# A decoder layer on one Trainium2 core: a room for the first down weights, scores over 128 rows, and a reordered norm

## The chip, the cores and the metric

The kernel runs on one core of a Trainium2 chip. The metric is the time of one execution on the device, in microseconds (us); lower is better. A core has five engines with a queue of instructions each: PE (TensorE, matrix products), DVE (VectorE), ACT (ScalarE), POOL (GpSimd) and SP (SyncE, which here issues nearly all DMAs). An engine takes its instructions in the order in which they stand in its queue, and an instruction waits by semaphores for the results and buffers of other engines.

## The reference

One layer of a decoder for 520 columns: 512 positions of a prompt and one new position each of 8 running sequences. The model has width 1024. Two feed-forward parts of hidden width 2816 enclose a mixer.

```python
def half_ffn(x, g, w1, w3, w2):
    h = rmsnorm(x, g)
    return x + 0.5 * ((jax.nn.silu(h @ w1) * (h @ w3)) @ w2)

def trunk_layer(x, ffn1, mixw, ffn2, past):
    g_mix, w_in, conv_w, g_conv, g_attn, w_out = mixw
    x = half_ffn(x, *ffn1)
    h = rmsnorm(x, g_mix)
    ...
    y_c = rmsnorm(b_g * conv_out, g_conv)
    y_a = rmsnorm(attn.reshape(attn.shape[:2] + (ATTN_WIDTH,)), g_attn)
    x = x + jnp.concatenate([y_c, y_a], axis=-1) @ w_out
    x = half_ffn(x, *ffn2)
    return x, state
```

In the mixer `h @ w_in` gives the three inputs of a gated convolution (512 channels) and q, k, v of 8 heads of 64. The prompt's attention adds up three dilated windows, and the 8 running sequences look into a cache of 1024 positions, which is also copied to the output with the new rows. A last norm closes the program.

## The kernel before

All activations lie transposed: 1024 rows in 8 tiles `X` of 128 partitions, 520 columns in two halves of 260. A float32 operand is split into a high and a low part of a shorter format, and a product takes three matrix products (`mm3`, lines 121 to 123): high by high, high by the activation's low part, low by high. `load_w` (L95) brings a block of weights into `raw` by DMA, ACT makes `hi` of it (L108) and DVE makes `lo` (L109). `hi` and `lo` have three buffers each, `raw` four.

**Feed-forward parts** (`ffn`, L225). The first four hidden tiles are made with plain products, the other 18 in pairs (`pair`, L318), where `seven` (L366) forms two output tiles with seven products in place of eight, from sums of weight blocks; the sums' high and low parts are the tiles `hs` and `ls` in the pool `su` (L382), with two buffers each. The hidden tiles are `hh` and `hl` (L305, L334). The down projection `down` (L412) is run after the hidden tiles 0 to 3, 4 to 13 and 14 to 21 (`CUTS`), each time over all 8 output tiles, with its own weights from `load_w`, which it adds into `X`. Behind the last pair, `preload()` (L73) loads ACT's table that holds both logarithm and exponential. The Silu of the hidden tiles (L301, L324) uses another table; where an ACT function isn't in the table loaded last, the build puts a load ahead of it.

**Mixer.** Weights for the first three projections are loaded ahead (`ahead`, L497), then the operand `mh`, `ml` and the squares are made, and `rstd_rows` (L164) makes the norm's factor: it adds up the squares by a product with ones, DVE forms the mean (L182), ACT takes a logarithm and an exponential (L183, L184), and DVE refines the result (L185 to L187). The projections q, k, v, the convolution's parts, the heads and the cache's products run in an order written by hand (`ORDER`, L33); a timeline scheduler then mixes what is ready. `head` (L578) makes the scores of one head in eight products: four with 128 rows, in which the key tile `k2` holds its high part in one half of the rows and its low part in the other and the query's high part `q2` stands in both, and four with 64 rows for the query's low part `ql` with the key's high part. `rstd` (L189) is a norm by columns for the convolution's group (step R), with `rstd_columns` (L146) and `spread` (L157); `rstd_rows` once more is the attention group's norm (`r2`, L813), which `out_proj` needs at L771.

**End.** The second `down` with `finish` (L820) makes the last tiles half by half; each half runs `rstd_columns`, whose logarithm and exponential are L150 and L151, then `give` (L845): `spread`, the products with the norm's factor on DVE and POOL, and the DMAs out.

## Time and profile before

| | us |
|---|---|
| median of three runs | 1001.39 (1000.5 to 1004.54) |
| the profiled execution | 1001.53 |
| its span in the trace | 999.7 |
| PE busy | 977.4 (98%) |
| DVE busy | 719.6 (72%) |
| ACT busy | 519.9 (52%) |
| POOL busy | 69.7 (7%) |

The first feed-forward part lasts until about 373 us, the mixer until about 622, the second feed-forward part until about 977, and the last norm to the end. In the rows of a timeline, the first number is the start, the second the duration; a bracket at the end tells how long the engine had been idle and who ended that. The durations of PE's products overlap, so the distance of their starts is what counts.

### The profile page before, as it was taken

How to read it: one execution, taken by the hardware profiler on the slowest of the kernel's cores; microseconds unless marked ns; L12 is line 12 of the kernel's file. 1: busy time of each engine (PE TensorE's matmuls, PEld its weight loads, DVE VectorE, ACT ScalarE, POOL GpSimd, SP SyncE). 2: the span in 40 equal slices, each digit the busy share in tenths (PEclk: the TensorE clock that was granted, in tenths of full speed). 3: DMA queues.
4: the chain of work that ended last, by engine and by line, in shares of the span. 5: the costliest groups of instructions: out<-in, count | busy, mean ns of one | idle time of the engine just before them, and what ended most of it. 6: DMA issues, size and time to landing. Idle time of an engine off the chain costs nothing.

```text
span 999.7 us, 19200 instructions
## 1 busy us (share of the span) xinstructions
PE 977.4 (98%) x7897; PEld 955.6 (96%) x7897; DVE 719.6 (72%) x1153; ACT 519.9 (52%) x941; POOL 69.7 (7%) x89
## 2 busy tenths in 40 slices
PE   8999999999999999999999999999999999999997
PEld 8999999999999999999999899999999999999997
DVE  7889987336886446667788899769988634788432
ACT  5536665324665446667566555435656422565442
POOL 1000000000000131112022210000000000000022
PEclk9999999999999999999999999999999999999998
DMA  7344343445444444243146565325443233333302
GB/s 243 110 137 164 133 147 123 163 138 173 145 147 130 165 157 149 89 145 138 65 152 228 197 225 191 108 94 179 149 147 127 80 93 104 106 107 106 106 22 86
DMA packets 37912, 136.62 MB, mean 137 GB/s; under 512 B 5760, under 2 KB 8512, under 8 KB 37312
## 3 DMA queue, kind: packets, MB, share of 16 engines
q1 hardware_dynamic: 37824, 135.39, 39.9%
q8 instruction: 62, 1.02, 0.4%
q14 instruction: 26, 0.21, 0.1%
HBM read 131.07 MB, written 37.82 MB: 169 GB/s over the span
## 4 chain that ended last, share of the span: by engine, by line
PE 78%; DVE 11%; DMA 5%; issue 3%; ACT 2%; POOL 1%; SPq 0%; POOLq 0%; DVEq 0%; ACTq 0%
PE ps L121 24%; PE ps L123 24%; PE ps L122 24%; DVE lo L390 2%; DMA raw<-in_w3a 2%; PE s L589 1%; DMA raw<-in_w1a 1%; DVE ls L390 1%; DVE lo L109 1%; DMA raw<-in_w1b 1%; DVE raw L377 1%; PE pt L610 1%; DVE ws L378 1%; DVE ws L376 1%; DVE ws L375 1%
## 5 line engine op out<-in xcount | busy, mean ns | idle before, releaser
L108 ACT ACTIVATE hi<-raw 128x1024 fp32r<-128x1024 f32 (+3 forms) x136 | 119.0, 878 | 208.3 <-PE ps L122 162.7
L121 PE MATMUL ps<-hh,hi 128*128 128x260 f32 x704 | 198.4, 284 | 3.4 <-ACT hi L108 1.4
L123 PE MATMUL ps<-hh,lo 128*128 128x260 f32 x704 | 198.8, 284 | 1.2 <-DVE lo L109 1.2
L122 PE MATMUL ps<-hl,hi 128*128 128x260 f32 x704 | 198.2, 282 | 0.1
L109 DVE TENSOR_TENSOR lo<-raw,hi 128x1024 fp32r<-128x1024 f32 (+3 forms) x136 | 138.6, 1020 | 76.3 <-ACT hi L108 75.0
L121 PEld LDWEIGHTS ps<-hh,hi 128*128 128x128 f32 x704 | 132.3, 189 | 4.9 <-ACT hi L108 1.8
L123 PEld LDWEIGHTS ps<-hh,lo 128*128 128x128 f32 x704 | 132.2, 188 | 2.1 <-DVE lo L109 1.6
L122 PEld LDWEIGHTS ps<-hl,hi 128*128 128x128 f32 x704 | 132.6, 188 | 0.4 <-DVE hl L305 0.3
L121 PE MATMUL ps<-mh,hi 128*128 128x260 f32 x384 | 110.1, 287 | 1.7 <-DVE q L518 1.1
L123 PE MATMUL ps<-mh,lo 128*128 128x260 f32 x384 | 109.4, 285 | 0.2 <-DVE u L643 0.2
L122 PE MATMUL ps<-ml,hi 128*128 128x260 f32 x384 | 109.3, 285 | 0.0
L389 ACT ACTIVATE hi<-raw 128x512 fp32r<-128x512 f32 x144 | 82.9, 622 | 37.2 <-PE ps L122 27.9
L390 DVE TENSOR_TENSOR lo<-raw,hi 128x1024 fp32r<-128x1024 f32 x72 | 87.8, 1219 | 7.2 <-ACT hi L389 6.9
L123 PE MATMUL ps<-f1sh,lo 128*128 128x260 f32 x288 | 81.6, 285 | 1.8 <-DVE lo L390 1.7
L121 PE MATMUL ps<-f0sh,hi 128*128 128x260 f32 x288 | 81.8, 284 | 1.4 <-ACT a L405 1.0
L121 PE MATMUL ps<-f1sh,hi 128*128 128x260 f32 x288 | 81.5, 283 | 0.7 <-ACT a L405 0.5
L123 PE MATMUL ps<-f0sh,lo 128*128 128x260 f32 x288 | 81.3, 285 | 0.7 <-DVE lo L390 0.6
L122 PE MATMUL ps<-f0sl,hi 128*128 128x260 f32 x288 | 81.2, 282 | 0.0
L122 PE MATMUL ps<-f1sl,hi 128*128 128x260 f32 x288 | 81.1, 282 | 0.0
L144 POOL TENSOR_TENSOR acc<-acc,sq 128x520 f32<-128x520 f32 (+1 forms) x19 | 28.9, 1523 | 741.4 <-ACT sq L143 737.5
L121 PEld LDWEIGHTS ps<-mh,hi 128*128 128x128 f32 x384 | 72.4, 189 | 2.8 <-issue 1.8
L122 PEld LDWEIGHTS ps<-ml,hi 128*128 128x128 f32 x384 | 72.4, 188 | 1.1 <-issue 0.7
(278 smaller groups left out, 2664.5 us busy)
## 6 DMA issues: line engine op xcount, KB each, us to landing
out_cko<-in_ck SPq DMA_DIRECT2D x16, 1023.0 KB, 6.8
out_cvo<-in_cv SPq DMA_DIRECT2D x16, 1023.0 KB, 6.8
raw<-in_w_in SPq DMA_DIRECT2D x24, 512.0 KB, 3.3
raw<-in_w1b SPq DMA_DIRECT2D x22, 512.0 KB, 3.3
raw<-in_w3b SPq DMA_DIRECT2D x22, 512.0 KB, 3.3
raw<-in_w3a SPq DMA_DIRECT2D x21, 512.0 KB, 3.3
raw<-in_w1a SPq DMA_DIRECT2D x20, 512.0 KB, 3.3
raw<-in_w2a SPq DMA_DIRECT2D x16, 320.0 KB, 2.9
```

The lines of the kernel that those rows point to most:

```text
L108: A.activation(hi, raw, AF.Copy)
L109: V.tensor_tensor(lo, raw, hi.bitcast(F32), ALU.subtract)
L121: PE.matmul(out, lhsT=hi, rhs=xh, start=start, stop=False, skip_group_check=more)
L122: PE.matmul(out, lhsT=hi, rhs=xl, start=False, stop=False, skip_group_check=more)
L123: PE.matmul(out, lhsT=lo, rhs=xh, start=False, stop=stop, skip_group_check=more)
L144: eng.tensor_tensor(dst[:, c], dst[:, c], sq[:, c], ALU.add)
L375: V.tensor_tensor(s[:, 0], rb[:, :KQ], rb[:, KQ:], ALU.add)
L376: V.tensor_tensor(s[:, 1], s[:, 0], ra[:, :KQ], ALU.add)
L377: V.tensor_tensor(rb[:, :KQ], rb[:, :KQ], ra[:, :KQ], ALU.add)
L378: V.tensor_tensor(s[:, 2], s[:, 1], ra[:, KQ:], ALU.add)
L389: A.activation(h[:, c:c + KQ], f[:, c:c + KQ], AF.Copy)
L390: V.tensor_tensor(l, f, h.bitcast(F32), ALU.subtract)
```

## The change

- `load_w` can be given a `room`, two tiles into which it puts `hi` and `lo`. After the pairs of the second and the third group, `ffn` takes two more tiles of the pool `su`, of the size and tags of `hs` and `ls`, and loads the first weights of the following down projection into them (`down_weights`), ahead of `down`, and in the third group ahead of `preload()`.
- After the first four hidden tiles, the output tiles 0 and 1 run together (`late`): the products with the first three hidden tiles for both, then with the fourth for both.
- The scores take, for the query's low part too, 128 rows: each head's low part stands in a tile of 128 rows, of which the other 64 are zero. There are four such tiles, zeroed once by POOL, and each holds its half in turn. The eight products stand in plain order.
- The mixer's third weight is loaded behind the exponential of the norm. The zeros of `pth`, `ptl` and `sq2` are written by POOL; the tiles `sqm` of the cache's products share the slots of `q2`, and are taken once.
- In `ORDER`, step B0 comes ahead of q2.

```diff
-ORDER = ("A0 C00 C01! k1 q1 q2 B0 v1 v2 t1 C02 A1! B1! k3 k2 t2 A2 v3 C10 C11 q3 B2 t3 A3 C12 "
+ORDER = ("A0 C00 C01! k1 q1 B0 q2 v1 v2 t1 C02 A1! B1! k3 k2 t2 A2 v3 C10 C11 q3 B2 t3 A3 C12 "
...
-    def load_w(src, n, cuts=None, then=None):
+    def load_w(src, n, cuts=None, then=None, room=None):
         raw = wp.tile([P, n, P], F32, name="raw", tag="raw", bufs=4)
-        hi = wp.tile([P, n, P], F32R, name="hi", tag="whi")
-        lo = wp.tile([P, n, P], F32R, name="lo", tag="wlo")
+        hi, lo = room or (wp.tile([P, n, P], F32R, name=x, tag=f"w{x}") for x in ("hi", "lo"))
...
-        A.activation(out, out, AF.Exp, scale=-0.5)
+        power = A.activation(out, out, AF.Exp, scale=-0.5)
...
+        return power
...
-                for m, then in zip((0, 1, 4, 5, 2, 6, 3, 7), (sum_x, None, sum_x) + 5 * (None,)):
-                    down(w2, 0, CUTS[1], Hh, Hl, psum_tile, ms=(m,))
+                for ms, then in zip(((0, 1), (4,), (5, 2, 6, 3, 7)), (sum_x, sum_x, None)):
+                    down(w2, 0, CUTS[1], Hh, Hl, psum_tile, ms=ms, late=len(ms) == 2)
...
                 for m in range(c0, c1, 2):
                     pair(m)
+                room = [su.tile([P, 12, P], F32R, name=x, tag=x) for x in ("hs", "ls")]
+                first = down_weights(w2, c0, c1, 0, room)
                 if c1 < KF:
-                    down(w2, c0, c1, Hh, Hl, psum_tile)
+                    down(w2, c0, c1, Hh, Hl, psum_tile, first=first)
             preload()
...
-            down(w2, CUTS[-2], KF, Hh, Hl, psum_tile, finish)
+            down(w2, CUTS[-2], KF, Hh, Hl, psum_tile, finish, first=first)
...
+    def down_weights(w2, k0, k1, m, room=None):
 
         n = k1 - k0 if k1 - k0 <= KD else (k1 - k0) // 2
+        return [tuple(load_w(w2[m, :, k:k + n], n, room=room and [t[:, k - k0:k - k0 + n] for t in room])) + (k, n)
+                for k in range(k0, k1, n)]
...
+        if late:
+            ws, ps = [parts(m) for m in ms], [psum_tile() for m in ms]
+            for a, b in ((0, k1 - k0 - 1), (k1 - k0 - 1, k1 - k0)):
+                with tc.issue_after(PE_last()) if a else ExitStack():
+                    for w, p in zip(ws, ps):
+                        gemm(p, w, Hh, Hl, of=(a, b))
...
-            ahead = [load_w(w_in[mt], KD) for mt in (20, 12, 16)]
+            ahead = [load_w(w_in[mt], KD) for mt in (20, 12)]
...
-            rstd_rows(two, sums, D, rbc)
+
+            with tc.issue_after(rstd_rows(two, sums, D, rbc).ins):
+                ahead.append(load_w(w_in[16], KD))
...
-                V.memset(t[:, 0:128].bitcast(F32), 0.0)
+                G.memset(t[:, 0:128].bitcast(F32), 0.0)
...
+            rest = [[ap.tile([P, S], F32R, name=f"ql{i}{e}") for e in range(2)] for i in range(2)]
+            for r in rest:
+                for e in range(2):
+                    G.memset(r[e][ROWS[1 - e]].bitcast(F32), 0.0)
...
-                    V.tensor_tensor(ql[ROWS[e]], q[ROWS[e], :S], q2[e][ROWS[e]].bitcast(F32), ALU.subtract)
+                    V.tensor_tensor(ql[e][ROWS[e]], q[ROWS[e], :S], q2[e][ROWS[e]].bitcast(F32), ALU.subtract)
...
-                for at_, (ib, low) in enumerate(((0, 0), (1, 0), (0, 1), (1, 1), (2, 1), (2, 0), (3, 0), (3, 1))):
+                for ib in range(4):
...
-                    mm = PE.matmul(dst[ib], lhsT=ql[rows, i] if low else q2[e][:, i], rhs=k2[e][rows if low else slice(0, P), :n],
-                                   start=at_ in (0, 4, 6), stop=one or at_ in (5, 7), skip_group_check=one and at_ > 0)
...
+                    PE.matmul(dst[ib], lhsT=q2[e][:, i], rhs=k2[e][:, :n], start=True, stop=False)
+                    PE.matmul(dst[ib], lhsT=ql[e][:, i], rhs=k2[e][:, :n], start=False, stop=True)
...
+                if not zeroed:
+                    zeroed.extend(ap.tile([P, HP * 130 + 64], F32R, name=f"sqm{i}", tag=f"q2{i}", bufs=2) for i in range(2))
```

How instructions stand after the change is shown in three places. The line numbers of the new kernel differ by up to some twenty from those above. ACT, last pair of the first feed-forward part, before: L324 to L326 are the last pair's Silu, L397 to L405 its copies out of PSUM, L108 the first weights of the down projection, L334 the last hidden tiles, L75 the preload.

```order
L334 ACTIVATE hh_3625<-b 128x520
L389 ACTIVATE hi<-raw 128x512 x2
L324 ACTIVATE a<-a 128x520
L399 ACTIVATE b<-ps 128x260
...
L401 ACTIVATE b<-ps 128x260
L108 ACTIVATE hi<-raw 128x1024
L326 ACTIVATE a<-ps 128x260
L108 ACTIVATE hi<-raw 128x1024
L334 ACTIVATE hh_3875<-b 128x520
L405 ACTIVATE b<-ps 128x260
L108 ACTIVATE hi<-raw 128x1024
L334 ACTIVATE hh_3879<-b 128x520
L75 ACT_TABLE_LOAD
```

The same place now (L107 is the old L108; L391, L401, L403 and L407 are the old L389, L399, L401 and L405):

```order
L407 ACTIVATE b<-ps 128x260
L107 ACTIVATE hs<-raw 128x1024
L75 ACT_TABLE_LOAD
L403 ACTIVATE a<-ps 128x260
L391 ACTIVATE hi<-raw 128x512 x2
L334 ACTIVATE hh_3623<-b 128x520
L391 ACTIVATE hi<-raw 128x512 x2
L401 ACTIVATE b<-ps 128x260
L324 ACT_TABLE_LOAD
L324 ACTIVATE a<-a 128x520
```

The first weights now go to `hs`, ahead of the last pair's copies; the preload has moved with them, and the Silu brings a load of its own. The second feed-forward part reads alike.

ACT, the attention group's norm, before (L183 and L184 are its logarithm and exponential):

```order
L108 ACTIVATE hi<-raw 128x512
L171 ACTIVATE rhi<-acc_a 128x520
L108 ACTIVATE hi<-raw 128x512 x2
L183 ACTIVATE r_4475<-rv_7207 128x520
L184 ACTIVATE r_4475<-r_4475 128x520
L108 ACTIVATE hi<-raw 128x512 x2
```

The same place now (each line number is one less):

```order
L107 ACTIVATE hi<-raw 128x512
L170 ACTIVATE rhi<-acc_a 128x520
L107 ACTIVATE hi<-raw 128x512 x2
L182 ACT_TABLE_LOAD
L182 ACTIVATE r_4473<-rv_7207 128x520
L183 ACT_TABLE_LOAD
L183 ACTIVATE r_4473<-r_4473 128x520
L107 ACTIVATE hi<-raw 128x512 x2
```

Two table loads have come in; the same two stand at the norm ahead of the mixer, at the convolution's norm, at the norm ahead of the second feed-forward part, and twice at the last norm. In all, ACT has 19 table loads now, where it had 5.

PE, the first head's scores, before (`s01`, `s2` and `s3` are the sums of query blocks 0 and 1, 2, and 3):

```order
L589 MATMUL s01_4688<-k20_4668,q20_4599 128x256 x2
L589 MATMUL s01_4688<-k20_4668,ql_4601 128x256 x2
L589 MATMUL s2_4689<-k20_4668,ql_4601 128x384
L589 MATMUL s2_4689<-k20_4668,q20_4599 128x384
L589 MATMUL s3_4690<-k20_4668,q20_4599 128x512
L589 MATMUL s3_4690<-k20_4668,ql_4601 128x512
```

The same place now:

```order
L610 MATMUL s01_4693<-k20_4673,q20_4605 128x256
L611 MATMUL s01_4693<-k20_4673,ql00_4484 128x256
L610 MATMUL s01_4693<-k20_4673,q20_4605 128x256
L611 MATMUL s01_4693<-k20_4673,ql00_4484 128x256
L610 MATMUL s2_4694<-k20_4673,q20_4605 128x384
L611 MATMUL s2_4694<-k20_4673,ql00_4484 128x384
L610 MATMUL s3_4695<-k20_4673,q20_4605 128x512
L611 MATMUL s3_4695<-k20_4673,ql00_4484 128x512
```

High and low parts take turns now, all with the full tile `ql00`; in the other heads other products stand between some of the eight, in both kernels.

## Rows read from the trace of the kernel before

**Rows 1.** The page, part 1: each engine's busy time, share, instructions.
```profile
PE 977.4 (98%) x7897; PEld 955.6 (96%) x7897; DVE 719.6 (72%) x1153; ACT 519.9 (52%) x941; POOL 69.7 (7%) x89
```
**Rows 2.** Busy time by stretch: PE, PEld, DVE, ACT, POOL; PE's clock; DMA.
```profile
60.00:115.00 55.00, 54.15 (x446) 53.51 (x447) 53.58 (x78) 31.63 (x59) 0.00 (x0) 1.00 0.46 159
400.00:575.00 175.00, 174.35 (x1332) 162.96 (x1330) 134.05 (x286) 109.32 (x209) 32.43 (x54) 1.00 0.42 146
977.00:1000.00 23.00, 16.84 (x146) 16.37 (x145) 7.00 (x24) 5.33 (x14) 4.64 (x7) 0.83 0.28 94
```
**Rows 3.** Timeline of PE, the first head's scores: start, duration, instruction.
```profile
405.92 0.40 PE L589 MATMUL s<-k,q 128*128 128x256 f32 x2
...
407.46 0.49 PE L589 MATMUL s<-k,ql 64*128 64x512 f32 x1
407.88 0.40 PE L121 MATMUL ps<-mh,hi 128*128 128x260 f32 x1
408.11 0.29 PE L122 MATMUL ps<-ml,hi 128*128 128x260 f32 x1
```
**Rows 4.** Timeline of PE, products of 512 columns over 128 rows.
```profile
420.40 0.40 PE L619 MATMUL o<-pth,v 128*128 128x512 f32 x1
420.64 0.39 PE L621 MATMUL o<-ptl,v 128*64 128x512 f32 x1
```
**Rows 5.** Timeline of PE: its waits at the down projections of the first part.
```profile
59.87 0.39 PE L121 MATMUL ps<-hh,hi 128*128 128x260 f32 x1 [0.92 <-ACT hh L305]
...
188.96 0.39 PE L121 MATMUL ps<-hh,hi 128*128 128x260 f32 x1 [0.71 <-ACT hi L108]
...
323.67 0.39 PE L123 MATMUL ps<-hh,lo 128*128 128x260 f32 x1 [0.61 <-DVE lo L109]
...
330.00 0.39 PE L121 MATMUL ps<-hh,hi 128*128 128x260 f32 x1 [0.52 <-DVE b L330]
```
**Rows 6.** Timeline of ACT: table loads, and what follows one of them.
```profile
331.00 1.28 ACT L75 ACT_TABLE_LOAD   x1
...
641.31 1.28 ACT L301 ACT_TABLE_LOAD   x1
642.60 0.64 ACT L301 ACTIVATE a<-a 128x520 f32<-128x520 f32 x1
```
**Rows 7.** Timeline of ACT at the norm ahead of the mixer.
```profile
382.59 1.06 ACT L108 ACTIVATE hi<-raw 128x1024 fp32r<-128x1024 f32 x1 [4.59 <-PE ps L122]
...
384.57 0.62 ACT L184 ACTIVATE rbc<-rbc 128x520 f32<-128x520 f32 x1
```
**Rows 8.** Timeline of PE, mixer's start, and a product behind the attention's norm.
```profile
385.63 0.28 PE L121 MATMUL ps<-mh,hi 128*128 128x260 f32 x1
...
393.07 0.36 PE L121 MATMUL ps<-mh,hi 128*128 128x260 f32 x1 [1.07 <-DVE q L518]
...
399.71 0.36 PE L121 MATMUL ps<-mh,hi 128*128 128x260 f32 x1 [0.62 <-DVE k L518]
...
603.48 0.36 PE L121 MATMUL ps<-Yh,hi 128*128 128x260 f32 x1
```
**Rows 9.** Timeline of ACT at the attention group's norm.
```profile
597.75 0.63 ACT L108 ACTIVATE hi<-raw 128x512 fp32r<-128x512 f32 x1 [2.72 <-PE ps L122]
598.29 0.62 ACT L183 ACTIVATE r<-rv 128x520 f32<-128x520 f32 x1
598.95 0.64 ACT L184 ACTIVATE r<-r 128x520 f32<-128x520 f32 x1
```
**Rows 10.** Timeline of DVE: the first use of that norm.
```profile
602.64 0.70 DVE L771 TENSOR_TENSOR t<-ps,r 128x520 f32<-128x520 f32 x1
```
**Rows 11.** Waits of PE: who is waited for, us in all, times, longest.
```profile
PE nps L160 <- DVE rr L154: 0.3, 1, 0.3
```
**Rows 12.** Timeline of ACT: the last norm's two logarithms.
```profile
983.81 0.20 ACT L150 ACTIVATE rr<-rv 65x4 f32<-65x4 f32 x1 [2.20 <-DVE rv L149]
...
990.59 0.20 ACT L150 ACTIVATE rr<-rv 65x4 f32<-65x4 f32 x1 [0.37 <-DVE rv L149]
```

More of the change, by code (lines that the diff above doesn't have):

```diff
@@ L410, in seven, with down @@
         return px
-    def down(w2, k0, k1, Hh, Hl, psum_tile, finish=None, ms=range(KD)):
+    def down_weights(w2, k0, k1, m, room=None):
         n = k1 - k0 if k1 - k0 <= KD else (k1 - k0) // 2
+        return [tuple(load_w(w2[m, :, k:k + n], n, room=room and [t[:, k - k0:k - k0 + n] for t in room])) + (k, n)
+                for k in range(k0, k1, n)]
+    def down(w2, k0, k1, Hh, Hl, psum_tile, finish=None, ms=range(KD), first=None, late=False):
         def parts(m):
-            return [load_w(w2[m, :, k:k + n], n) + (k, n) for k in range(k0, k1, n)]
+            return first if first and not m else down_weights(w2, k0, k1, m)
         def update(m, ps, h):
@@ L429, in whole @@
                 finish(m, None)
+        if late:
[4 more added lines that the diff above has]
+                        gemm(p, w, Hh, Hl, of=(a, b))
+            for m, p in zip(ms, ps):
+                V.scalar_tensor_tensor(halves(X[m]), p[:, :, :TH], 0.5, halves(X[m]), ALU.mult, ALU.add)
+            return
         for m in ms[:-2] if finish else ms:
@@ L560, in do_q @@
                 q2 = [ap.tile([P, S], F32R, name=f"q2{e}", tag=f"q2{e}", bufs=2) for e in range(2)]
-                ql = ap.tile([P, S], F32R, name="ql", tag="ql", bufs=2)
+                ql = rest[hp % 2]
                 for e in range(2):
@@ L583, in head @@
                 dst = [s01[:, 0:256], s01[:, 256:512], s2_[:, 0:384], s3_[:, 0:512]]
-                for at_, (ib, low) in enumerate(((0, 0), (1, 0), (0, 1), (1, 1), (2, 1), (2, 0), (3, 0), (3, 1))):
+                for ib in range(4):
                     n = max(256, P * (ib + 1))
                     i = slice(ib * P, (ib + 1) * P)
-                    one = ib < 2
-                    mm = PE.matmul(dst[ib], lhsT=ql[rows, i] if low else q2[e][:, i], rhs=k2[e][rows if low else slice(0, P), :n],
-                                   start=at_ in (0, 4, 6), stop=one or at_ in (5, 7), skip_group_check=one and at_ > 0)
-                    if at_ not in (0, 6):
-                        tc.keep_in_program_order(mm)
+                    PE.matmul(dst[ib], lhsT=q2[e][:, i], rhs=k2[e][:, :n], start=True, stop=False)
+                    PE.matmul(dst[ib], lhsT=ql[e][:, i], rhs=k2[e][:, :n], start=False, stop=True)
                 mx = sm.tile([P, 4], F32, name="mx", tag="mx")
@@ L658, in conv @@
                 yield
+            zeroed = []
             def padded(n):
-                z = [ap.tile([P, HP * 130 + 64], F32R, name=f"sqm{i}", tag=f"sqm{i}") for i in range(2)]
-                for t in z:
+                if not zeroed:
+                    zeroed.extend(ap.tile([P, HP * 130 + 64], F32R, name=f"sqm{i}", tag=f"q2{i}", bufs=2) for i in range(2))
+                for t in zeroed:
                     G.memset(t[:, :n].bitcast(F32), 0.0)
-                return z
+                return zeroed
             def sample_scores():
@@ L670, in sample_scores @@
                 q2 = ap.tile([P, B, HP, 2], F32, name="sq2")
-                V.memset(q2, 0.0)
+                G.memset(q2, 0.0)
                 for e in range(2):
```

## The prediction

> **What bounds the kernel now.** I read the busy times first, then the stages, then the waits of PE (TensorE), and only then single instructions. PE is busy for 977.4 of 999.7 us, DVE (VectorE) for 719.6 and ACT (ScalarE) for 519.9 [rows 1]. By stage, PE is full in the attention stage too, 174.35 of 175 us, while DVE and ACT have 41 and 66 us free there; in the first pairs of the first feed-forward part (60 to 115 us) DVE has only 1.4 us free of 55; the last 23 us are the one stretch in which PE is not the bound (16.84 us) [rows 2]. So a saving must take time out of PE's own steps or out of one of its few waits, and a new cost counts where it stands on a chain that PE or the end waits for. A product of 128x260 takes PE about 0.12 us from start to start, and the durations of 0.28 us in the rows overlap; I go by starts.
>
> The profiled run took 1001.53 us, 1.83 us of it outside the span of 999.7, and I keep these 1.83. The median of the three runs is 1001.39, so the sum against the profiled run stands for the median too. About 0.5% (5 us) is what a measurement of this kernel can tell from no change.
>
> **Scores over 128 rows.** One head has eight score products, which now alternate between 128 rows of the array and 64. The first head shows the price: from the start at 405.92 to the second product behind the scores at 408.11 are 2.19 us [rows 3]. Eight plain products of these widths and one of 260 columns would take less: 256 columns go by at 0.12 us, 512 columns over 128 rows take 0.24 (420.40 to 420.64) [rows 4], and 384 lie between at 0.18. That is 4 x 0.12 + 2 x 0.18 + 2 x 0.24 + 0.12 = 1.44 us. The difference is 0.75 us a head, and the rows say where it is: the 64-row product of 512 columns is followed after 0.42 us, not 0.24, and the next one after 0.23, not 0.12 [rows 3]. Eight heads: -6.0 us. In heads whose scores stand scattered among projections there are one or two more switches, so -7 is the far end. The other end is half of it, -3, if the heads become bound by what follows the scores: PE comes 0.75 us earlier to a chain on DVE and ACT which is busy 77% and 62% of that stage [rows 2]. I take -5.5, near the full price, since PE hardly waits there today (0.65 us in 175) and the free time of DVE is 5 us a head. The low parts of q now go into two tiles with the same number of subtractions, so DVE has no more to do; the zeros of four tiles 64x512 are POOL's (GpSimd's), which is 7% busy [rows 1].
>
> **First weights in the sums' room.** At the end of the second and the third group of pairs the first weights of the down projection find their buffer taken by the last pair's, and PE waits for their conversion: 0.71 us for ACT at 188.96, 0.61 us for DVE at 323.67, 0.52 us for the last hidden tile at 330.00 [rows 5]. The second feed-forward part shows all three again with the same lengths. With a second place for these weights, the products of hidden tiles that are long ready run ahead of the last pair's, so the first two waits have their cover and the third is shortened by 18 products (18 x 0.12 = 2.2 us, of which the last pair's chain takes back most). Per part I count 0.8 us at the second group (between 0.3 and 1.0) and 1.0 at the third (1.4 if all goes; against nothing, below): twice, -1.6 and -2.0.
>
> **The table preload moves on ACT, as a consequence.** ACT loads a function table in 1.28 us, when the load's turn comes in its queue: at 331.00 behind all of the last pair's work, and at 641.31 straight ahead of the Silu at 642.60 that needs it [rows 6]. In the order of before, the preload of the table with both logarithm and exponential comes after the last hidden tile. In the new order it stands behind the conversion of the new first weights, ahead of the last pair's Silu, in both parts. That Silu then brings its own load, the preload is spent, and every logarithm and exponential behind it gets a load of its own: 19 loads in place of 5. The 14 new ones are 14 x 1.28 = 18 us of ACT. I go through them:
> - Two ahead of the last pairs' Silu, with the preload now ahead of copies that PE waits for. ACT has gaps there, so the new weights' gain of 1.4 becomes the 1.0 above; at worst it eats it (+0.2 a part).
> - The norm ahead of the mixer, two. The first falls into idle time. The second is exposed, but the third weight's conversion no longer stands before the logarithm, which gives back some 0.6 us. PE waits there today 1.07 and 0.62 us, later on (393.07, 399.71) [rows 8]. Now the third weight's conversion (382.59, 1.06 us) comes behind the exponential (384.57) [rows 7], which itself is done some 0.7 us later (1.28 - 0.6): it would run from 385.2, and DVE's low part from 386.6 to 387.8, where PE wants both from 385.63 on [rows 8]. That is about 2 us in one wait, in place of 1.7 in two: +0.3, between -0.6 and +1.5.
> - The column norm of the convolution: one hidden, the other with some cover by products that PE has ahead of the result: +0.1, between 0 and 0.5.
> - The row norm of the attention group. The logarithm follows a conversion without a gap (597.75, then 598.29), and the exponential follows at 598.95 [rows 9]. DVE's first use of the result runs from 602.64 to 603.34 [rows 10], and PE's product that needs the buffer which this use frees starts at 603.48 [rows 8]: no slack. Both loads are in the open: 2 x 1.28 = +2.5. DVE has little free here, so I take the full price; the low end is one load, +1.2.
> - The norm ahead of the second feed-forward part, two: its result is first used on a whole product of 1024 rows, which PE still has to make: 0.
> - The final norm, twice two. First half: ACT is idle for 2.20 us before the logarithm at 983.81 [rows 12], so the load is hidden; the exponential's is not, and PE waits today already 0.3 us for this very result [rows 11], so the last products start 1.15 to 1.28 later; I take 1.15. Second half: ACT is idle for 0.37 us before the logarithm at 990.59 [rows 12], so its load costs 1.28 - 0.37 = 0.9, then the exponential's 1.28 in full. Nothing but the end hangs on it: 1.15 + 0.9 + 1.28 = +3.3, between 2.6 and 3.5.
>
> **The late last tile and the rest.** After the first four hidden tiles, PE waits 0.92 us for the last of them (59.87) [rows 5]. The pair of output tiles that runs three quarters of each sum first puts 18 more products ahead of that, so this wait goes. But the pairs that follow are bound by DVE, which has 1.4 us free in 55 [rows 2]: PE will arrive early and wait there. I take 0, and -1.3 as the other end. DVE's zeros moved to POOL are 0.5 us that DVE loses in a stage where they stand ahead of the norm; they are in the mixer's -0.6. The first pairs' products stand in another order; I see no sign in it and allow 1.5 us either way.
>
> **The sum.** -5.5 -1.6 -2.0 +0.3 +0.1 +2.5 +3.3 +0 = -2.9 us: a span of 996.8, and 998.6 us for the run.
>
> **The rivals.**
> (a) The loads find cover. If the row norm's and the tail's logarithm find their table loaded in time, and PE takes up the rest in the stage behind, then only one exponential's 1.28 in the tail stays: -5.5 -3.6 + 1.3 = -7.8, and with the late tile's 1.3 it is -9.1: 992 to 994 us. For it: ACT is idle for half of the span. Against it: at these two places the rows stand without a gap. Chance 0.17.
> (b) The scores' gain doesn't arrive. If DVE and ACT set the pace of the heads, half the 6 us is lost to waits for the score rows' maxima, and with everything else as forecast the time is 1001.5 - 2.9 + 2.5 = 1001, up to 1004.7 if the two weights' places gain nothing either (+3.6). For it: DVE is at 77% with chains of eight steps behind each score; against it: PE waits so little there. Chance 0.13.
> (c) Slower: the 14 loads are on the path in full. They cost 18.0 us against gains of 9.1: +8.9, some 1010 us; it decides from 11 loads in the open (11 x 1.28 - 9.1 = 5.0). For it: the new loads stand between instructions that depend on each other, and ACT's queue behind them holds the conversions of weights. Against it: five of the 14 fall into gaps by the rows, or before results that are needed late. Chance 0.05.
> (d) A load holds ACT for longer than its row, because the engine first has to finish what it has. At twice the 1.28 us, the six loads that I count in the open (one at the mixer, two at the row norm, three in the tail) would cost 6 x 1.28 = 7.7 us more: 1006.3. Against it: the load at 641.31 is followed by its Silu 1.29 us later, with nothing between [rows 6]. Chance 0.03. By the Trainium skill, "ScalarE: Activation LUTs", What ACT_TABLE_LOAD costs, a switch is about 2.66 us, 1283 ns for the load and some 1380 ns for a drain; as an estimate from that page the sum would come to about 1007 us. The trace agrees with its first figure and shows nothing of the second.
>
> **How the numbers follow.** The forecast has 0.62, (a) 0.17, (b) 0.13, (c) 0.05 and (d) 0.03. By itself the forecast spans 995.5 to 1002.5. Below 996.4 (faster by over 0.5%) lie (a) and an eighth of the forecast: 0.25. Above 1006.4 lie (c) and half of (d), and a little of (b) with (d): 0.08. Within 0.5%: 0.67. The range goes from 993, which halves (a), to 1004, near the upper end of (b); I leave some 0.08 below it and 0.1 above.
>
> **What would show it.** Right: 19 loads on ACT; a score group without steps over 0.24 us; PE's waits at 188.96, 323.67 and their twins gone; a PE wait of some 2.5 us at the row norm's first products and a last stretch some 3 us longer from its first logarithm to the end. Wrong: the heads' stage (400 to 575 us) shortened by less than 3 us, which would put (b) in place of the first term; DVE waiting less than 1.3 us at the row norm, which is (a); waits of PE for weights' conversions behind the loads, which is (c).

## The result, and the profile after

The changed kernel takes 1010.05 us (median) against 1002.25 for the one before: a ratio of 1.008, 95% interval 1.0062 to 1.0099, so 8 us slower, between 6 and 10. The prediction said 998.6 us, 2.9 us faster, in a range of 993 to 1004. It was wrong in sign. The profiled execution took 1010.05 us with a span of 1008.2.

The busy times answer to [rows 1]. PE has less to do than before (975.7 us, not 977.4), in a span that is 8.5 us longer; ACT has 17.5 us more, close to the 17.9 of 14 table loads of 1.28 us. The page's part 1 of the changed kernel, busy time by engine:

```profile
PE 975.7 (97%) x7897; PEld 957.9 (95%) x7897; DVE 717.1 (71%) x1150; ACT 537.4 (53%) x955; POOL 75.0 (7%) x96
```

So PE is idle for 10 us more in sum. The waits of PE in the changed kernel, costliest first (who is waited for: us in all, times, longest); four of them are new or have grown by over 1.5 us:

```profile
PE nps L159 <- DVE rr L153: 3.8, 2, 2.5
PE ps L122 <- DVE lo L392: 3.6, 4, 1.7
PE ps L122 <- DVE lo L108: 3.4, 5, 1.1
PE ps L120 <- ACT a L403: 2.9, 4, 1.3
PE ps L120 <- DVE t L793: 2.8, 2, 2.3
PE ps L120 <- DVE X L433: 2.0, 1, 2.0
```

The first is the last norm's factor (0.3 us before, [rows 11]); the fourth is a copy out of PSUM that stands behind the preload at the ends of the hidden stages; the fifth is the first use of the attention group's norm; the sixth is an update of `X` behind the first four hidden tiles, near 77 us. Here is the fifth, on ACT (timeline of the changed kernel: start, duration, instruction), answering to [rows 9]:

```profile
596.55 0.63 ACT L107 ACTIVATE hi<-raw 128x512 fp32r<-128x512 f32 x1 [2.72 <-PE ps L121]
597.20 1.28 ACT L182 ACT_TABLE_LOAD   x1
598.50 0.64 ACT L182 ACTIVATE r<-rv 128x520 f32<-128x520 f32 x1
599.15 1.28 ACT L183 ACT_TABLE_LOAD   x1
600.45 0.64 ACT L183 ACTIVATE r<-r 128x520 f32<-128x520 f32 x1
```

Both loads lie in the open, each with the function behind it 1.30 us after the load's start, as the prediction had it; nothing of the longer hold of rival (d) shows. And here is PE at the product that waits for this norm, with the products before and behind it:

```profile
602.10 0.28 PE L122 MATMUL ps<-Yh,lo 128*128 128x260 f32 x1
604.64 0.42 PE L120 MATMUL ps<-Yh,hi 128*128 128x260 f32 x1 [2.26 <-DVE t L793]
604.86 0.42 PE L121 MATMUL ps<-Yl,hi 128*128 128x260 f32 x1
...
607.89 0.42 PE L120 MATMUL ps<-Yh,hi 128*128 128x260 f32 x1
608.11 0.33 PE L121 MATMUL ps<-Yl,hi 128*128 128x260 f32 x1
...
608.40 0.29 PE L120 MATMUL ps<-Yh,hi 128*128 128x260 f32 x1
```

The wait is 2.3 us, close to the 2.5 that the prediction put there. What it did not have is the next 3.5 us: 16 products go by at 0.217 us from start to start instead of 0.12, which costs 16 x 0.097 = 1.55 us more. The stretch's granted clock is lower in step with them. Busy time by stretch of the changed kernel (PE, PEld, DVE, ACT, POOL; PE's granted clock; DMA):

```profile
600.00:610.00 10.00, 7.74 (x52) 7.56 (x52) 7.18 (x12) 4.29 (x8) 0.00 (x0) 0.83 0.30 106
```

0.83 over these 10 us is a part at 1.2 and the rest at 2.4 GHz. Before, PE was granted 1.00 everywhere ahead of its last ten microseconds. In the last norm, too, the loads lie in the open (ACT of the changed kernel, its second half, answering to the second of [rows 12]):

```profile
995.41 0.51 ACT L863 ACTIVATE X<-X,gv 128x260 f32<-128x260 f32 x1
995.94 1.28 ACT L149 ACT_TABLE_LOAD   x1
...
997.46 1.28 ACT L150 ACT_TABLE_LOAD   x1
```

PE's products that use the two results, in the kernel before and then in the changed one:

```profile
985.32 1.00 PE L160 MATMUL nps<-ident,rr 65*128 65x65 f32 x8
991.66 3.09 PE L160 MATMUL nps<-ident,rr 65*128 65x65 f32 x16 [0.30 <-DVE rr L154]
```

```profile
990.93 1.10 PE L159 MATMUL nps<-ident,rr 65*128 65x65 f32 x8 [1.25 <-DVE rr L153]
999.59 3.67 PE L159 MATMUL nps<-ident,rr 65*128 65x65 f32 x16 [2.52 <-DVE rr L153]
```

The waits are 1.25 and 2.52 us where there were none and 0.30. The clock is a smaller part here: it was already low at this place before ([rows 2], 0.83 over the last 23 us), and the 16 products take 3.67 us instead of 3.09.

### The profile page after: what moved, and what is told of

It reads as the page before. It is cut to its first block, busy times and chain, and to the rows that moved or that the text cites. A ratio compares the mean times of both kernels' runs of the same rounds, so it can differ in the third digit from the quotient of the medians.

```text
span 1008.2 us, 19207 instructions
## 1 busy us (share of the span) xinstructions
PE 975.7 (97%) x7897; PEld 957.9 (95%) x7897; DVE 717.1 (71%) x1150; ACT 537.4 (53%) x955; POOL 75.0 (7%) x96
## 4 chain that ended last, share of the span: by engine, by line
PE 77%; DVE 10%; DMA 4%; issue 4%; ACT 4%; POOL 1%; SPq 0%; POOLq 0%; DVEq 0%; ACTq 0%
PE ps L120 25%; PE ps L122 25%; PE ps L121 24%; DVE lo L108 2%; DVE lo L392 2%; DMA raw<-in_w1b 1%; DMA raw<-in_w1a 1%; DMA raw<-in_w3b 1%; ACT hi L107 1%; DMA raw<-in_w_out 1%; DVE raw L379 1%; DVE ls L392 1%; PE pt L629 1%; DVE ws L380 1%; DVE ws L378 1%
## 5 line engine op out<-in xcount | busy, mean ns | idle before, releaser
L107 ACT ACTIVATE hi<-raw 128x1024 fp32r<-128x1024 f32 (+3 forms) x130 | 113.2, 877 | 182.8 <-PE ps L121 141.8
L120 PE MATMUL ps<-hh,hi 128*128 128x260 f32 x632 | 178.8, 285 | 1.1 <-ACT hi L107 0.6
L122 PE MATMUL ps<-hh,lo 128*128 128x260 f32 x632 | 178.7, 284 | 0.0
L121 PE MATMUL ps<-hl,hi 128*128 128x260 f32 x632 | 178.3, 283 | 0.0
L108 DVE TENSOR_TENSOR lo<-raw,hi 128x1024 fp32r<-128x1024 f32 (+3 forms) x130 | 132.0, 1019 | 62.4 <-ACT hi L107 62.1
L120 PEld LDWEIGHTS ps<-hh,hi 128*128 128x128 f32 x632 | 119.4, 190 | 2.3 <-ACT hi L107 1.8
L122 PEld LDWEIGHTS ps<-hh,lo 128*128 128x128 f32 x632 | 119.2, 189 | 0.6 <-DVE lo L108 0.5
L121 PEld LDWEIGHTS ps<-hl,hi 128*128 128x128 f32 x632 | 119.6, 189 | 0.0
L391 ACT ACTIVATE hi<-raw 128x512 fp32r<-128x512 f32 x144 | 82.8, 622 | 36.0 <-PE ps L121 29.2
L122 PEld LDWEIGHTS ps<-mh,lo 128*128 128x128 f32 x384 | 72.2, 188 | 3.9 <-DVE lo L108 3.2
```

Of the source, the lines that this page charges most:

```text
L107: A.activation(hi, raw, AF.Copy)
L108: V.tensor_tensor(lo, raw, hi.bitcast(F32), ALU.subtract)
L120: PE.matmul(out, lhsT=hi, rhs=xh, start=start, stop=False, skip_group_check=more)
L121: PE.matmul(out, lhsT=hi, rhs=xl, start=False, stop=False, skip_group_check=more)
L122: PE.matmul(out, lhsT=lo, rhs=xh, start=False, stop=stop, skip_group_check=more)
L391: A.activation(h[:, c:c + KQ], f[:, c:c + KQ], AF.Copy)
```

## The experiments

Each ran beside the kernel before on the same chip; ratios are to that kernel. The groups 1 to 4, 5 to 8, 9 to 12 and 13 to 14 had medians of 1001.96, 1002.13, 1003.38 and 1002.09 us for it, so kernels of two groups are compared by their ratios. The theory after the two traces was that the 14 loads are the loss and are dearer than their rows; the rival was that the loads cost what the prediction said, and the late last tile and the order of the products the rest.

**1. The changed kernel without the new loads.**

```diff
                 for m in range(c0, c1, 2):
                     pair(m)
+                if c1 == KF:
+                    preload()
                 room = [su.tile([P, 12, P], F32R, name=x, tag=x) for x in ("hs", "ls")]
...
-            preload()
             sx.close()
```

> The changed kernel with one move: the table preload is issued ahead of the new first weights, so that it stands behind the last hidden tile again; 5 table loads in place of 19, all else as changed. Theory T (the 14 loads are the loss, and dearer than their rows because PE's clock falls behind long waits): the stretches that the loads lengthened in the trace of the changed kernel go back: about 2.5 + 2.6 us at the row norm and behind it, 4.3 in the last norm, 1.5 at the mixer's start, about 1.4 at the end of each hidden stage, some 13 us: 997 us, 0.5% faster than before. Rival U (the loads cost only what the prediction said, some 6 us, and the rest is the late last tile and the reordered products): 1004 us.

998.38 us, a ratio of 0.9967 (0.9947 to 0.9987): 11.7 us less than the changed kernel (11.3 by the ratios), and faster than before. So the loads cost nearly the 13 us of the theory, and the change without them is worth 3.3 us.

**2. The loads alone, on the kernel before.**

```diff
                 for m in range(c0, c1, 2):
+                    if m + 2 == KF:
+                        preload()
                     pair(m)
...
-            preload()
             sx.close()
```

> The kernel before with the table preload issued ahead of the last pair, so that it has 19 table loads too and nothing else of the change. Theory T: 10 to 13 us slower than before, with the row norm 5 us and the last norm 4 us longer, and a lower granted clock behind the row norm. Rival U: 6 us slower (2.5 at the row norm, 3.3 in the last norm, nothing elsewhere). If loads find cover: within 2 us of before.

1013.78 us, 1.0122 (1.01 to 1.0143): 12.2 us slower, from both sides nearly the same price. In the trace the row norm's product waits 2.26 us for DVE again, and its 10 us behind that are granted 0.85. PE's last product ahead of the wait, the one that waits and the second feed-forward part's first, then the busy time by stretch:

```profile
607.13 0.28 PE L123 MATMUL ps<-Yh,lo 128*128 128x260 f32 x1
609.68 0.56 PE L121 MATMUL ps<-Yh,hi 128*128 128x260 f32 x1 [2.26 <-DVE t L772]
...
629.55 0.36 PE L121 MATMUL ps<-f1h,hi 128*128 128x260 f32 x1 [0.51 <-DVE t L772]
```

```profile
600.00:610.00 10.00, 7.74 (x64) 7.56 (x63) 7.34 (x13) 5.63 (x7) 0.00 (x0) 0.98 0.52 181
610.00:620.00 10.00, 10.00 (x73) 10.00 (x73) 8.40 (x15) 4.82 (x8) 0.00 (x0) 0.85 0.31 112
```

**3. The scores alone, on the kernel before.** The edit is that of the scores, the cache's zeroed tiles in `q2`'s slots and the one step of `ORDER` in the diff of the change; its core:

```diff
-                ql = ap.tile([P, S], F32R, name="ql", tag="ql", bufs=2)
+                ql = rest[hp % 2]
...
+                    PE.matmul(dst[ib], lhsT=q2[e][:, i], rhs=k2[e][:, :n], start=True, stop=False)
+                    PE.matmul(dst[ib], lhsT=ql[e][:, i], rhs=k2[e][:, :n], start=False, stop=True)
```

> The kernel before with the scores over 128 rows alone (four zeroed tiles for the query's low part, eight products in plain order, the cache's zeroed tiles in the slots of the query's, B0 ahead of q2 in the order, which these slots need). By the prediction's first term 5.5 us faster than before, 400 to 575 us shortened by it, the first head's eight products and the next in 1.44 us instead of 2.19. If the heads are bound by DVE and ACT instead: 3 us or less.

996.7 us, 0.9951 (0.9931 to 0.997): 4.9 us faster, between 3.0 and 6.9. PE's timeline of the first head in this kernel, answering to [rows 3]:

```profile
408.40 0.28 PE L592 MATMUL s<-k,q 128*128 128x256 f32 x1
...
409.22 0.39 PE L592 MATMUL s<-k,q 128*128 128x512 f32 x1
409.45 0.40 PE L593 MATMUL s<-k,ql 128*128 128x512 f32 x1
409.68 0.29 PE L121 MATMUL ps<-mh,hi 128*128 128x260 f32 x1
409.80 0.28 PE L122 MATMUL ps<-ml,hi 128*128 128x260 f32 x1
```

From 408.40 to 409.80 are 1.40 us where the prediction said 1.44 and the kernel before took 2.19. The step behind the last score is 0.23 again, and the one behind the next product 0.12. The whole stage answers as well: from PE's 3150th product (396 us in the kernel before) to its 4650th (594 us) this kernel takes 192.5 us and the kernel before 198.1, so 5.6 us less.

**4. The late last tile alone, on the kernel before.** The edit is the `late` branch of `down` and the lines that call it:

```diff
-                for m, then in zip((0, 1, 4, 5, 2, 6, 3, 7), (sum_x, None, sum_x) + 5 * (None,)):
-                    down(w2, 0, CUTS[1], Hh, Hl, psum_tile, ms=(m,))
+                for ms, then in zip(((0, 1), (4,), (5, 2, 6, 3, 7)), (sum_x, sum_x, None)):
+                    down(w2, 0, CUTS[1], Hh, Hl, psum_tile, ms=ms, late=len(ms) == 2)
```

> The kernel before with the late last tile alone (output tiles 0 and 1 of the first down projection together, three quarters of both sums first). Theory T leaves it at 0 (the prediction's term): within 1 us of before. Rival U: 2 to 3 us slower, with a wait of PE of about 2 us near 77 us and a lower granted clock behind it, as in the trace of the changed kernel.

1006.64 us, 1.0044 (1.0023 to 1.0064): 4.4 us slower. Here theory T fell, and rival U held for the late tile, which is dearer than its 2 to 3 us; with runs 1 and 2, both causes are real. PE's timeline of this kernel near 77 us:

```profile
76.99 0.28 PE L122 MATMUL ps<-f0sl,hi 128*128 128x260 f32 x1
79.23 0.58 PE L121 MATMUL ps<-f0sh,hs 128*128 128x260 f32 x1 [1.96 <-DVE X L427]
79.61 0.42 PE L122 MATMUL ps<-f0sl,hs 128*128 128x260 f32 x1
79.83 0.59 PE L123 MATMUL ps<-hh,lo 128*128 128x260 f32 x1
80.21 0.42 PE L121 MATMUL ps<-hh,hi 128*128 128x260 f32 x1
```

The wait of 0.92 us at 59.87 is gone, as predicted. PE comes earlier, as predicted, and waits 2 us for DVE 17 us later; then its clock falls here too (0.87 granted from 80 to 90 us), and some 12 products go by at 0.217.

**5. Neither loads nor late tile.** The changed kernel with the edit of experiment 1 and the output tiles of the first down projection one by one, as before:

```diff
-                for ms, then in zip(((0, 1), (4,), (5, 2, 6, 3, 7)), (sum_x, sum_x, None)):
-                    down(w2, 0, CUTS[1], Hh, Hl, psum_tile, ms=ms, late=len(ms) == 2)
+                for m, then in zip((0, 1, 4, 5, 2, 6, 3, 7), (sum_x, None, sum_x) + 5 * (None,)):
+                    down(w2, 0, CUTS[1], Hh, Hl, psum_tile, ms=(m,))
```

> The changed kernel with the preload behind the last pair and without the late last tile (output tiles one by one again). If the two causes found so far, the 14 loads and the late tile, are separate and all of the loss: the 998.4 us with the loads taken away, less the 4.4 us that the late tile alone cost: about 994 us, 0.8% faster than before. If the late tile costs only beside the old order of the rest: 998 us again.

994.5 us, 0.9923 (0.9901 to 0.9944): within the intervals the two causes add up and are all of the loss. This is the fastest kernel of the study, 7.7 us faster than before.

**6. Does the clock make the row norm dearer? A first try.** On the kernel of experiment 2:

```diff
+                    if k0 and m == 2:
+                        fill = psS.tile([P, 512], F32, name="fill", tag="s")
+                        with tc.issue_after(PE_last()):
+                            keep_warm(24, fill)
+                        with tc.issue_after(PE_last()):
+                            gemm(ps, [(hi, lo, k0, 4)], Yh, Yl)
```

> The kernel with the preload ahead of the last pair (19 loads, no other change), with 24 products of ones (128 columns each, some 2.6 us) put into PE's queue ahead of the product that waits at the row norm; their sum is used by nobody. Theory C (behind that wait PE's granted clock falls, and this, not the wait itself, makes 1.5 of the 3.9 us there): the granted clock of the next 20 us stays at 1.00, and the stretch from the row norm to the second part's first hidden tile is 1.0 to 1.5 us shorter than without the products, though they add work. Rival W (the wait and DVE's backlog behind it are the whole cost): no shorter, or longer by some tenths.

1015.85 us, 1.0129 (1.0104 to 1.0154). The products of ones took 5.3 us, not 2.6: each stands as two in the trace (48 records). The clock stayed at 1.00 there, but they were 2.7 us longer than the wait, so the kernel's time settles nothing, and the run was repeated as 9. Its trace already leans to theory C: from the last product ahead of the wait to the second part's first one are 23.95 us (608.34 to 632.29) against run 2's 22.42, only 1.5 us more, so some 1.2 us came back behind the products of ones.

**7. The late tile in the first part alone.**

```diff
+                plan = ((0, 1), (4,), (5, 2, 6, 3, 7)) if i == 0 else ((0,), (1,), (4,), (5, 2, 6, 3, 7))
```

> The kernel before with the late last tile in the first feed-forward part alone. If the cost of 4.4 us is the wait near 77 us and the lower clock behind it, all or nearly all of it is here: 3.5 to 4.4 us slower than before. If it comes from the second part's other order of products: within 1.5 us of before.

1004.15 us, 1.0015 (1.0001 to 1.003): 1.5 us slower, not 3.5, although PE's wait near 77 us is 2.88 us in this trace and the clock falls behind it (0.84 granted from 80 to 90 us). A miss of the expectation: the wait that can be pointed at is not the whole cost, and the second part has its share. What that is, single traces don't show: between 686 and 815 us PE waits 3.5 us for low parts of weights from DVE in run 4 and 1.7 in the kernel before, but 2.9 in run 3, which has no late tile.

**8. The rooms alone, with the preload in its place.** On the kernel before:

```diff
+                if c1 == KF:
+                    preload()
+                room = [su.tile([P, 12, P], F32R, name=x, tag=x) for x in ("hs", "ls")]
+                first = down_weights(w2, c0, c1, 0, room)
                 if c1 < KF:
-                    down(w2, c0, c1, Hh, Hl, psum_tile)
-            preload()
+                    down(w2, c0, c1, Hh, Hl, psum_tile, first=first)
```

> The kernel before with the rooms for the first down weights alone, and the preload behind the last hidden tile (5 table loads). The prediction's terms for them, without what the loads take: -1.6 at the second groups and up to -2.8 at the third: 997.5 to 998.5 us. By the traces of the runs so far, in which the second groups gain nothing and the third some 2 us each: 998 us as well, with all of it at the third groups. If it gains nothing: 1002.

999.4 us, 0.9963 (0.9949 to 0.9977): 3.7 us faster. The traces say where. PE of this kernel at the second group's end, answering to the second of [rows 5]:

```profile
186.54 0.39 PE L120 MATMUL ps<-f0sh,hi 128*128 128x260 f32 x1 [0.52 <-DVE b L405]
...
191.72 0.39 PE L120 MATMUL ps<-hh,hi 128*128 128x260 f32 x1 [0.23 <-ACT hi L107]
```

0.75 us in two waits stand where 0.71 stood in one: nothing gained. At the third group's end, PE of this kernel has no wait that the timeline names between 312 and 335 us, where [rows 5] had 0.61 and 0.52. All of the gain is there and at its twin in the second part: counted at the same products, PE gains 1.7 us at each.

**9. The clock at the row norm, with fewer products.** As 6, with 11 in place of 24:

```diff
-                            keep_warm(24, fill)
+                            keep_warm(11, fill)
```

> As the run with 24 products of ones at the row norm, with 11 of them, since a product of ones stood for twice the time that I had counted (24 took 5.3 us): 11 take some 2.4 us, about the wait. Theory C (PE's clock falls behind the wait and makes 1.5 of the 3.9 us): granted clock 1.00 from 600 to 620 us, and from the row norm to the second part's first hidden tile 1.0 to 1.5 us less than in the kernel with 19 loads alone; in all 1012.5 us against its 1013.8. Rival W (wait and backlog are all): the same stretch, 1013.8 us.

1012.56 us, 1.0102 (1.0079 to 1.0124), by the ratios 2.0 us less than run 2. The intervals of the two runs overlap, so the reading rests on the traces. PE of this kernel at the same place:

```profile
608.05 0.29 PE L123 MATMUL ps<-Yh,lo 128*128 128x260 f32 x1
608.17 2.62 PE L86 MATMUL fill<-ones 128*128 128x128 f32 x22
610.59 0.36 PE L121 MATMUL ps<-Yh,hi 128*128 128x260 f32 x1
610.78 0.29 PE L122 MATMUL ps<-Yl,hi 128*128 128x260 f32 x1
...
629.45 0.39 PE L121 MATMUL ps<-f1h,hi 128*128 128x260 f32 x1 [1.15 <-ACT hi L108]
```

and its busy time by stretch:

```profile
600.00:610.00 10.00, 10.00 (x87) 10.00 (x86) 7.37 (x14) 5.63 (x7) 0.00 (x0) 1.00 0.55 183
610.00:620.00 10.00, 9.98 (x84) 9.80 (x83) 9.06 (x15) 4.97 (x9) 0.00 (x0) 1.00 0.40 133
```

PE has the same 2.4 us to bridge, spends them on products that nobody needs, keeps 1.00, and the next products go by at 0.12. From the last product ahead of the wait the sixteenth behind it comes 1.5 us sooner than in run 2, and the second part's first one 1.0 us sooner (21.40 us, 608.05 to 629.45, against 22.42), at the lower end of what theory C expected. So at the row norm the loads cost the wait and, apart from it, the clock behind the wait.

**10 and 11. Is it PE's order that makes the late tile dear?** With the late tile, the first pair's second product had moved ahead of 22 products of the down projection. It was held behind them, on the kernel before with the late tile (10) and on the changed kernel with the preload in its place (11):

```diff
+        with tc.issue_after(behind) if behind else ExitStack():
+            product(pw, hs[:, 0], ls[:, 0], 3, True)
```

> The kernel before with the late last tile in both parts, and the first pair's second product (the one with the sums' weights) held behind the last product of the first down projection, where it stood before the change; with the late tile alone it had moved ahead of 22 of those. Theory O (PE waits 2 us near 77 us only because this product, which is not ready, stands ahead of 22 that are, 2.6 us of work): the wait at 77 us goes, with the lower clock behind it, and the 4.4 us shrink to 0 to 1.5. Rival D (DVE's backlog behind the two sums that end together is the loss): the wait only moves behind the 22 products, and the kernel stays 3 us or more slower than before.

> The changed kernel with the preload behind the last pair and with that product held in its old place: all parts of the change, without the two side effects. Theory O: 994 to 995.5 us, like the kernel without the late tile (994.5). Rival D: 997 us or more. Faster than 994 only if the late tile gains what it was made for, the 1.3 us wait near 59 us.

1005.79 us, 1.0035 (1.002 to 1.0049), and 998.96 us, 0.9962 (0.9946 to 0.9978): no better than without the hold (1.0044 and 0.9967). The order of PE isn't it: in run 10, PE starts the first of the 22 products 2.7 us after the one ahead of it, for its own low part comes as late from DVE.

**12. The norm ahead of the third weight.** Run 5 with the mixer's third weight loaded first again:

```diff
-            ahead = [load_w(w_in[mt], KD) for mt in (20, 12)]
+            ahead = [load_w(w_in[mt], KD) for mt in (20, 12, 16)]
...
-            with tc.issue_after(rstd_rows(two, sums, D, rbc).ins):
-                ahead.append(load_w(w_in[16], KD))
+            rstd_rows(two, sums, D, rbc)
```

> The changed kernel with the preload behind the last pair, without the late tile, and with the mixer's third weight loaded ahead of the norm again. It tells what the norm ahead of the third weight is worth when no table load stands in it: by the parts measured so far (scores -4.9, rooms -3.7, sum 993.5; with the reordered norm 994.5) it costs up to 1 us, and this kernel is at 993.5; by the prediction's bound it gains 0.6, and this one is at 995.

995.8 us, 0.9929 (0.991 to 0.9948). It can't be told from run 5. The reordered norm is worth nothing that can be measured in the time. With the loads it helps: counted at the same products, they cost 2.6 us at the mixer's start in run 2, which has the old order, and 1.4 in the changed kernel.

**13 and 14. Is it DVE's order?** The first pair's four weight sums on DVE were held behind the low part of the last down weights:

```diff
+        with tc.issue_after(behind) if behind else ExitStack():
             V.tensor_tensor(s[:, 0], rb[:, :KQ], rb[:, KQ:], ALU.add)
...
```

> The kernel before with the late last tile in both parts, and the first pair's four weight sums on DVE held behind the low part of the first down projection's last weights. With the late tile alone three of these sums had moved ahead of it, and one of them waits 0.8 us for its DMA; PE waits for that low part, or for the update of X beside it, whichever of PE's two orders is taken. Theory S (the order on DVE is the loss): DVE reaches that low part some 2 us earlier, PE's wait near 77 us shrinks to under 1 us, and the kernel is within 1.5 us of before. Rival F (the two halves of the first sums' low parts, 2 us each, stand ahead of it in any case and are made too late behind the two sums that end together): the wait stays near 2 us and the kernel 2 to 4 us slower than before.

> All parts of the change, with the preload behind the last pair and the same hold on DVE. Theory S: 994 to 995.5 us, like the kernel without the late tile. Rival F: 997 to 999 us.

1006.45 us, 1.0033 (1.0015 to 1.005), and 995.62 us, 0.9932 (0.991 to 0.9953). The wait at 77 us is gone in both, to 0.25 us from start to start (77.02 to 77.27) where 0.12 is usual. PE's order went back with it, but run 10 had that order too and kept the wait, so DVE's order did make it. By the ratios the hold gives back 3.5 us on the changed kernel (against run 1) and 1.1 on the kernel before (against run 4), each give or take nearly 3, so the two don't differ clearly. In the second part the same hold costs: between the same products (686 to 760 us in the kernel before) PE loses 2.7 us in run 13 and 2.0 in run 14, where it loses 0.8 in run 4. And the trace of run 13, an execution of 1009.62 us and so 3 us above its median, shows a long wait further on. PE and DVE of run 13:

```profile
165.19 0.59 PE L124 MATMUL ps<-f0sh,lo 128*128 128x260 f32 x1 [3.88 <-DVE lo L393]
```

```profile
161.98 0.69 DVE L378 TENSOR_TENSOR ws<-raw 128x512 f32<-128x512 f32 x1 [4.69 <-DMA raw<-in_w3a]
```

DVE waits 4.7 us for weights. The same instruction in the kernel before, on DVE, and what SP issued ahead of it there:

```profile
160.05 0.69 DVE L375 TENSOR_TENSOR ws<-raw 128x512 f32<-128x512 f32 x1 [0.78 <-DMA raw<-in_w3a]
```

```profile
151.82 0.33 SPq L113 DMA_DIRECT2D raw<-in_w3a  x1
152.20 0.52 SPq L465 DMA_DIRECT2D out_cko<-in_ck  x1
154.43 0.34 SPq L113 DMA_DIRECT2D raw<-in_w3a  x1
```

A copy of the cache, 1 MB, is queued between the two weight transfers of this pair, and the second is used from 160.05 on. In run 13 it comes to 161.98 with DVE ready earlier. In the kernel with the scores alone, which has no edit in this stage at all, DVE waits 2.64 us at the same instruction, and over the 16 traces of this study its wait lies between 0 and 4.7 us. So a single trace can't price anything that ends at this copy. That what is won ahead of it is waited away behind it is a reading of these traces; no run moved the copy.

## Why the prediction was wrong, point by point

The parts measured alone add up to the whole, and the prediction's steps can be held against them:

| part | predicted, us | measured alone, us |
|---|---|---|
| scores | -5.5 | -4.9 (-6.9 to -3.0) |
| rooms, without loads | -1.6 and -2.8 | -3.7 (-5.1 to -2.3) |
| the 14 loads | 0.8 + 0.3 + 0.1 + 2.5 + 3.3 = +7.0 | +12.2 (10.0 to 14.3) |
| late last tile | 0 | +4.4 (2.3 to 6.4) |
| sum | -2.9 | +8.0; the change: +8.0 (6.2 to 9.9) |

That the two last figures agree to a tenth is luck: the four intervals together leave the sum some 4 us either way.

**Right: the scores.** 0.75 us a head were predicted from the distance of starts, 0.79 measured at the first head (2.19 to 1.40), and the heads' stage is 5.6 us shorter in run 3, where -5.5 was the term. Rival (b) is out: no chain behind the scores took the gain.

**Right in place, wrong in size: the table loads.** That there are 19, where they stand, that a load takes its 1.28 us and nothing else, and that the six counted as open are open, all came as told; (a) and (d) are out. The step that failed is their price, +7.0 where 11.7 and 12.2 were measured. By place, from the starts of the same products of PE in the traces of the changed kernel and of run 1:

| place | predicted, us | traces, us |
|---|---|---|
| ends of the two hidden stages | +0.8 | +2.9 |
| mixer's start | +0.3, with some 0.6 given back by the third weight's new place | +1.4 |
| convolution's norm | +0.1 | +0.1 |
| row norm | +2.5 | +3.9 |
| norm ahead of the second part | 0 | 0 |
| last norm | +3.3 | +4.4 |
| sum | +7.0 | +12.7 |

At the row norm the prediction took the price of an open load as the time that its result comes later. This was right as the wait (2.3 us), and it left out the 1.55 us by which PE's products are slower behind it; run 9 shows that this is a cost of its own. In the last norm the sum had 1.15 and 2.2 us, and the waits of PE grew by 1.25 and 2.2; the rest is in the products behind the second wait, 0.6 us of it their lower clock. (The 0.3 us of [rows 11] that the prediction put to the first half is the second half's, at 991.66; it changes nothing.) At the ends of the hidden stages the load stands ahead of a copy that PE waits for, 1.29 us at 315.84, where the prediction let ACT's gaps take it:

```profile
313.03 1.06 ACT L107 ACTIVATE hs<-raw 128x1024 fp32r<-128x1024 f32 x1 [2.14 <-PE ps L121]
314.11 1.28 ACT L75 ACT_TABLE_LOAD   x1
315.40 0.39 ACT L403 ACTIVATE a<-ps 128x260 f32<-128x260 f32 x1
```

These are rows of ACT in the changed kernel: the conversion waits for its buffer until 313.03, not for its turn, so ACT's gap lies ahead of it and can't hide the load behind it. The prediction named ACT's gaps without a row, and did not ask where they end. Rival (c) was the outcome in sign, and its 1010 us are luck: it had all 14 loads in the open and gains of 9.1 us, where eight are in the open (the six, and one at each hidden stage's end: 10.2 us), the clock adds some 2 us, and the late tile costs 4.4 us.

**Wrong: the late tile at nothing.** The step was "the pairs that follow are bound by DVE ... I take 0, and -1.3 as the other end". That PE would arrive early and wait was right. That such a wait only gives back what was gained was wrong: DVE's order had moved with it (weight sums ahead of the last weights' low part), the wait became twice the one that was saved (1.96 us for 0.92), and behind it PE's clock fell. "I see no sign in it and allow 1.5 us either way" was said of the reordered products, and that 1.5 us was all that stood above zero; this and the loads' price put the range beside the result.

**Half right: the rooms.** The second groups' 0.8 us each did not come: the last pair's own wait took their place (0.52 and 0.23 us for 0.71). The third groups' did, with 1.7 us each where 1.4 was the most.

**What stays open.** By what mechanism the late tile costs in the second part: 4.4 us in both parts and 1.5 in the first alone leave it some 3 us (the intervals, 2.3 to 6.4 and 0.1 to 3.0, overlap), and run 4's trace shows no wait over 1.4 us and no lower clock there. Whether the hold on DVE is worth the same on both kernels. Waits behind cache copies differ by over 2 us between runs of kernels that are alike there, and I could not separate them. An order on SP that keeps the copies away from these weights wasn't tried.

## What to carry to other kernels

Look at what an edit does to the order on the engines that it doesn't name: here a preload that is tied to the instruction ahead of it moved with a new instruction, and an edit that gains 3.7 us by itself brought a loss of 12. Price a new wait of PE not by its length alone, but also with the products behind it, which may go by at the lower clock, and ask of every gap that is to hide something whether it lies ahead of the hidden work or behind it. A saving ahead of a stage that another engine or a transfer sets is not safely worth zero: here it came back as one longer wait.

## What the runs showed of the hardware

- PE's granted clock fell behind a single wait in the middle of full work. After waits of 2.3 us (row norm) and 2.0 us (77 us) the next 12 to 16 products of 128x260 went by at 0.217 us instead of 0.12, then at 0.12 again; at the row norm, with products of ones in the wait, they did not. The waits of 0.92 to 1.07 us of [rows 5, 8] left the clock at 1.00. It isn't the same in every run: in run 6 the stretch from 390 to 400 us, with the waits that the loads make at the mixer's start (1.08 and 1.75 us), was granted 0.77, in run 2 the same program with the same waits 1.00.
- A product of ones in full float32, 128x128 by 128 columns, takes PE about 0.22 us, two records each (11 in 2.4 us), while the split format's products of 260 columns take 0.12.
- A table load took 1.28 us in all 14 new places. In eleven of them the function behind it started 1.29 to 1.30 us after the load's start; in the other three its data came later (1.64 to 4.56 us after the load's start), and the load had run ahead of the data. So a load was hidden where ACT waited for its function's data, and not where the wait lay ahead of the load.
